# Attention stage of a hybrid decoder trunk: TensorE's instruction order fixed as the program is recorded, projections dealt anew over the steps

## The chip, the core and the metric

The kernel runs on one core of one Trainium2 chip. The metric is the device time of one execution in microseconds (us). An engine is named as the profile names it: PE is TensorE's matmuls, PEld its weight loads, DVE is VectorE, ACT ScalarE, POOL GpSimd, SP the queue that issues DMAs.

## What is computed

One layer of a trunk: adaLN-modulated RMSNorm, one input projection, two groups of 8 heads of 64 (an RWKV-7 recurrence and a causal stick-breaking attention), a gate on each, an output projection, residual and final RMSNorm, for 2048 tokens of width 1024 in float32. The change lies in the attention group:

```python
def block(args):                       # 128 queries of one head against all keys
    z = jnp.einsum('bhqd,bhkd->bhqk', q_blk, k).astype(jnp.float32) * scale
    mask = k_pos[None, :] < q_pos[:, None]
    log_1m = jnp.where(mask, jax.nn.log_sigmoid(-z), 0.0)
    after = lax.cumsum(log_1m, axis=3, reverse=True) - log_1m
    attn = jnp.where(mask, jnp.exp(jax.nn.log_sigmoid(z) + after), 0.0)
    return jnp.einsum('bhqk,bhkd->bhqd', attn.astype(v.dtype), v)
...
h = rmsnorm(x, norm_g[l]) * (1.0 + scale[:, None, :]) + shift[:, None, :]
p = h @ w_in[l]                        # q, k, v, the gates and the RWKV inputs
```

## The kernel before

The program has three parts in time. The first normalizes and transposes the input into `hth` and `htl` (high and low halves in fp16), the second is the attention, the third the RWKV recurrence and the output projection. Only the second is touched, and the end of the first.

**The attention is 16 steps.** Step n = 4j + b works on head pair j (4 pairs) and query block b (4 blocks of 512 rows); a group below is the four steps of one j. In a step there are 8(b+1) tiles of 128 queries by 512 keys, 8 of them on the diagonal and narrower. Per tile:
- `scores` (L506, L507): two matmuls into a PSUM bank z (3 banks); ACT makes two sigmoids u and s of it; DVE runs a scan over u (L519, L522); POOL multiplies s by it.
- `turn` (L535): four transposes of s into a bank tr (2 banks); ACT copies it to ah (L539), DVE takes the remainder al (L540).
- `weigh` (L553, L554): two matmuls by v add ah and al into the bank av (1 bank).

`attend` issues `scores` of a tile LEAD = 5 tiles ahead of its `turn`, and `weigh` LAG = 3 tiles behind.

**Beside it, `fill` makes the projections.** A projection is 24 matmuls of 512 columns (`inproj`; 96 of 128 columns for v) into one PSUM bank "mm", of which the stage has one. ACT and then DVE read the bank before the next projection may start. psk, psq, psv, psg and pss are the names of that bank by what is projected: k, q, v, a gate, an RWKV input. For q, ACT writes the high half (L419) and DVE the low half (L420) of the tile qt, and three DMAs (L422 to L424) move halves between partitions; the third overwrites what the first reads. `scores` of head 0 reads what the third wrote. `w_load` fetches the next projection's weights into a buffer "raw" (one of it) and takes their maximum on DVE (wm, L319); `w_split` scales and splits them, with a small matmul wtp (L333).

**What sets the order.** `_merge` interleaves `attend` and `fill` by the shares of work that their `yield`s name. That is the order of recording. The attention's context then has a scheduler (`schedule_with_timeline_sim=True`) that moves instructions on every engine by its own estimate; the engines run what comes out in order. Before the change nothing held TensorE to the order of recording, except that from step 12 on each first matmul of a k-step comes after the latest `weigh` (`pace`). Steps with b = 0 do not look ahead into the next step, and a step with b = 1 begins with five `scores`.

Of the kernel before, what the change touches and what calls it, by code (L numbers as in the profile page):

```python
# [7 lines left out]
F32 = mybir.dt.float32  # L8
# [10 lines left out]
P = 128  # L19
# [69 lines left out]
def trunk(nc, a, out):  # L89
# [7 lines left out]
    w_in, ada_w, w_out = a["w_in"][0], a["ada_w"][0], a["w_out"][0]  # L97

    base = -(-nc.sbuf_base // 32) * 32
    words = 23848  # L100
# [40 lines left out]
    crow = cp.tile([8, P], F32, name="crow")  # L141
# [12 lines left out]
    rows = cp.tile([P, P], F32, name="rows")  # L154
    col = {}
    r0 = 0
    for i, (nm, ap, off, n) in enumerate(vecs):
# [33 lines left out]
            xs.append(xt)  # L191
        xblk[b] = xs

    sbk = stage.enter_context(ExitStack())
    kp = sbk.enter_context(tc.tile_pool(name="kv", bufs=1))
    xctx = ExitStack()
# [128 lines left out]
    def w_split(kind, j):  # L325
        raw, m1 = W[kind, j]
        wh = wp.tile([P, KB, P], F16, tag="wh", name="wh")
        wl = wp.tile([P, KB, P], F16, tag="wl", name="wl")

        dg = wl.rearrange("p k c -> p (k c)")[:, 0:2 * P].bitcast(F32)  # L330
        A.activation(out=dg, in_=ident, func=AF.Copy, scale=m1)
        tp = tr_ps("wtp")
# [12 lines left out]
        rk = sm.tile([P, KB, 1], F32, name="rkw")  # L345
        V.tensor_scalar(out=rk[:, :, 0], in0=his, scalar1=ws, scalar2=None, op0=ALU.mult)
        (V if kind == "k" and j == 0 else G).tensor_tensor(out=raw, in0=raw, in1=_bc(rk, [P, KB, P]), op=ALU.mult)
        A.activation(out=wh, in_=raw, func=AF.Copy)
        V.tensor_tensor(out=wl, in0=raw, in1=wh, op=ALU.subtract)
        W[kind, j] = (wh, wl, uns)  # L350
        m = WCOL[kind][1]
        if m is not None:
            um = wp.tile([P, 1], F32, tag="um", bufs=8, name="um")
            u1 = wp.tile([P, 1], F32, tag="u1", bufs=8, name="u1")
            V.tensor_tensor(out=um, in0=uns, in1=vec("mu", 1, m + j), op=ALU.mult)
            V.tensor_tensor(out=u1, in0=uns, in1=mu1[:, m + j:m + j + 1], op=ALU.mult)
            W[kind, j] += (um, u1)
# [2 lines left out]
        w_load(kind, j, True)  # L360
        _run(w_split(kind, j))

    pace = [None]
# [12 lines left out]
    def inproj_tok(w, b, name):  # L376
        wh, wl = w[0], w[1]
        ps = mm_ps(name)
        for i in range(4):
            t = slice(i * P, (i + 1) * P)  # L380
            for k in range(KB):
                PE.matmul(ps[:, t], hth[b][:, k, t], wh[:, k], start=k == 0, stop=False)
                PE.matmul(ps[:, t], hth[b][:, k, t], wl[:, k], start=False, stop=False)
                PE.matmul(ps[:, t], htl[b][:, k, t], wh[:, k], start=False, stop=k == KB - 1)
                if k % 4 == 3:
                    yield 0.65
        return ps
# [73 lines left out]
    def combine(j, b, pool):  # L461
# [10 lines left out]
        yield 0.45  # L472
        tp = tr_ps()
        with tc.issue_after(first[0]) if first else nullcontext():
            for q in range(4):
# [19 lines left out]
    def scores(n, i, sb):  # L495
# [7 lines left out]
        nk = (q + 1) * P if diag else TB  # L503
        qs = slice(q * P, (q + 1) * P)
        z = z_ps()
        PE.matmul(z[:, 0:nk], qt[:, h, 0, qs], kt[:, h, 0:nk], start=True, stop=False)  # L506
        PE.matmul(z[:, 0:nk], qt[:, h, 1, qs], kt[:, h, 0:nk], start=False, stop=True)  # L507
# [20 lines left out]
    def turn(n, i, sb):  # L528
# [3 lines left out]
        q0 = ks if groups[gi][1] == b else 0  # L532
        tp = tr_ps()
        for q in range(q0, 4):
            PE.transpose(tp[:, q * P:(q + 1) * P], att[gi, q][:, ks * P:(ks + 1) * P], ident)  # L535
# [7 lines left out]
    def weigh(sb, n, i, ah, al, r):  # L543
# [9 lines left out]
        PE.matmul(av[:, r], vs, ah[:, r], start=first, stop=False, skip_group_check=True)  # L553
        ins = PE.matmul(av[:, r], vs, al[:, r], start=False, stop=last, skip_group_check=True)  # L554
        if n >= 12:
            pace[0] = ins.ins
        if last:

            if h == 0:
# [76 lines left out]
    w_load("g", 0, True)  # L636
    _merge((make_hs(*range(2, NB)), 3.6 * (NB - 2)), (proj_qkv(1), 15.6), (w_split("g", 0), 0.3))
    gate_row()
    xctx.close()
    cz = [zero1]  # L640

# [4 lines left out]

    def fill(n, sb):

        j, b = divmod(n, NB)
        end = j == NB - 1  # L650
        if n < 2:
            m = n + 2
        else:
            m = n + 1 if 2 < n < NST - 1 else None
        new = b == 3 and not end
        if b == 0 and j > 0:
            yield from w_split("g", j)
# [3 lines left out]
        if b == 3:  # L661
            yield from w_split("z" if end else "k", 0 if end else j + 1)
            w_load("rk" if end else "q", 0 if end else j + 1)
        gates = [("g", 0)], [("g", 1)], [("g", 2), ("g", 3), ("r", 0)], [("r", 1), ("r", 2), ("r", 3)]
        gates = [proj_g(kind, j, gb, sb) for kind, gb in gates[b]]
        if m is not None:
            yield from proj_k(m)
            if new:
                yield from gates.pop(0)
                yield from w_split("q", j + 1)  # L670
                w_load("v", j + 1)
            yield from proj_q(m)
            if new:
                yield from gates.pop(0)
                yield from w_split("v", j + 1)
                w_load("g", j + 1)
            yield from proj_v(m)
        if j > 0:
            yield from combine(j - 1, b, sb)
        if n == NST - 1:  # L680
            for i in range(4):
                yield from proj_z(i, sb)
                if gates:
                    yield from gates.pop(0)
                if i < 3:
                    yield from w_split(("rk", "rr", "rv")[i], 0)
                if i < 2:
                    w_load(("rr", "rv")[i], 0)
        for g in gates:
            yield from g  # L690
        if b == 1:
            w_load("r", j)

    def fill_work(n):
        b = n % NB
        if n == NST - 1:
            return 5.2 * 7 + 1.5
        return 5.2 * ((4, 4, 6, 6)[b] - 3 * (n == 2)) + 0.9 * (n > 3) + (0.2, 0, 0.2, 0.6)[b]

    dts = []  # L700
    early[0] = False
    with tc.tile_pool(name="sb", bufs=2) as sb:
# [7 lines left out]
        for n in range(NST):  # L710
            b = n % NB
            _merge((attend(n, sb), 8.6 + 10.48 * b), (fill(n, sb), fill_work(n)))
            if n == 1:
# [3 lines left out]
                for i in range(2):  # L717
                    dts.append(dram(f"dt{i}", [2, 2, 8, 65, 64]))
                    for m in range(2):
                        for h in range(2):  # L720
                            DMA.dma_start(out=dts[i][m, h].rearrange("c s t -> s c t")[0:64],
                                          in_=zeros[0:64].rearrange("p (c d) -> p c d", c=8))
    sbk.close()
    pace[0] = None


    HS = [slice(0, 64), slice(64, 128)]
# [608 lines left out]
```

## Time and profile before

| | |
|---|---|
| three runs | 1912.26, 1912.5 and 1915.36 us; median 1912.5 |
| the profiled execution | 1910.53 us, of which the span (first to last instruction) is 1908.8 |
| first `scores` / last `weigh` of the attention | 129.8 / 1034 us from the span's start |
| first matmul of the third part | 1044.9 us |
| PE, DVE, ACT, POOL busy over the span | 1719.8 (90%), 1348.7 (71%), 870.0 (46%), 754.6 (40%) us |
| mean granted TensorE clock | 0.971 of full speed |

All times of rows are microseconds from the span's start. A busy PE is one with a matmul in flight; matmuls overlap, so a row's duration is longer than the spacing of two matmuls. The granted clock has two levels, 2.4 GHz (1.00) and 1.2 GHz (0.50); a stretch shows their mean.

### The profile page before, as it was taken

To read this page: it belongs to the slowest core of one execution; us is meant where nothing else is said; L and a number is where in the kernel's file an instruction comes from. 1 tells how busy PE (TensorE), PEld (TensorE's weight loads), DVE (VectorE), ACT (ScalarE), POOL (GpSimd) and SP (SyncE) were. 2 spreads that over 40 slices of the span, in tenths; PEclk is the share of its full clock that TensorE was granted. 3 is DMA by queue.
4 is the path that set the end of the run, shared out by engine and by line. 5 is a ranking of instruction groups with operands and counts; after the bars stand their busy time and mean duration, and the time that the engine had idled before them with its cause. 6 is when DMAs were issued, how large, how long until landed. Compare 5 with 4: busy or idle time off the path is not lost. (4 is left out here: it accounts for less than half of the span.)

```text
span 1908.8 us, 38922 instructions
## 1 busy us (share of the span) xinstructions
PE 1719.8 (90%) x14880; PEld 1161.5 (61%) x14880; DVE 1348.7 (71%) x2855; ACT 870.0 (46%) x1718; POOL 754.6 (40%) x1106
## 2 busy tenths in 40 slices
PE   7979889999899998999997898898899888989998
PEld 2646556666566665667654455665555565667886
DVE  4876788577776778768775667877877777775542
ACT  2665567366654656546654333323332333422221
POOL 1425466355643646445444223222223232223322
PEclk9889999999999999999998899999999999999999
DMA  8442201222123221132111423222333333236442
GB/s 298 150 116 56 56 26 50 64 64 70 37 56 81 67 56 42 51 92 67 45 50 56 133 55 83 68 60 74 77 81 81 80 77 107 75 94 179 149 138 89
DMA packets 210408, 159.93 MB, mean 84 GB/s; under 512 B 113247, under 2 KB 171820, under 8 KB 210222
## 3 DMA queue, kind: packets, MB, share of 16 engines
q1 hardware_dynamic: 209220, 155.31, 29.2%
q8 instruction: 117, 1.92, 0.4%
q10 hardware_dynamic: 1002, 2.13, 0.4%
q14 instruction: 69, 0.57, 0.1%
HBM read 94.48 MB, written 44.04 MB: 73 GB/s over the span
## 5 line engine op out<-in xcount | busy, mean ns | idle before, releaser
L523 POOL TENSOR_TENSOR s<-s,u 128x512 f32<-128x512 f32 (+2 forms) x320 | 305.8, 963 | 216.5 <-ACT s L511 102.0
L540 DVE TENSOR_TENSOR al<-tr,ah 128x512 fp32r<-128x512 f32 (+1 forms) x320 | 187.4, 599 | 96.3 <-ACT ah L539 95.7
L522 DVE TENSOR_TENSOR_SCAN u<-u,dmask 128x512 f32<-128x512 f32 x192 | 240.0, 1268 | 13.0 <-ACT u L510 11.4
L539 ACT ACTIVATE ah<-tr 128x512 fp32r<-128x512 f32 (+1 forms) x320 | 171.7, 553 | 103.7 <-PE tr L535 99.6
L510 ACT ACTIVATE u<-z 128x512 f32<-128x512 f32 (+2 forms) x320 | 173.4, 555 | 73.4 <-PE z L507 49.0
L535 PE MATMUL tr<-kept_ident,s 128*128 128x128 f32 x1088 | 173.5, 279 | 33.1 <-DVE al L540 26.5
L511 ACT ACTIVATE s<-z 128x512 f32<-128x512 f32 (+2 forms) x320 | 166.2, 549 | 53.0 <-PE tr L535 53.0
L535 PEld LDWEIGHTS tr<-kept_ident,s 128*128 128x128 f32 x1088 | 130.3, 143 | 74.9 <-DVE al L540 38.4
L370 PE MATMUL pss<-kept_hh,kept_wh 128*128 128x512 f16 x416 | 161.3, 388 | 8.8 <-PEq L730 8.8
L372 PE MATMUL pss<-kept_hh,kept_wl 128*128 128x512 f16 x416 | 160.9, 387 | 0.0
L371 PE MATMUL pss<-kept_hl,kept_wh 128*128 128x512 f16 x416 | 160.9, 387 | 0.0
L372 PEld LDWEIGHTS <-kept_wl 128*128 128x128 f16 x928 | 93.2, 100 | 104.9 <-issue 14.2
L370 PEld LDWEIGHTS <-kept_wh 128*128 128x128 f16 x928 | 94.3, 102 | 101.4 <-issue 29.2
L371 PEld LDWEIGHTS <-kept_wh 128*128 128x128 f16 x928 | 93.0, 100 | 94.8 <-issue 25.0
L506 PE MATMUL z<-kt,qt 128*128 128x512 f32 (+2 forms) x320 | 132.1, 417 | 9.5 <-issue 3.7
L553 PE MATMUL av<-ah,vt 128*128 128x512 f32 (+1 forms) x320 | 136.5, 427 | 3.9 <-DVE o L564 2.3
L554 PE MATMUL av<-al,vt 128*128 128x512 f32 (+1 forms) x320 | 136.0, 426 | 0.2 <-DVE al L540 0.2
L507 PE MATMUL z<-kt,qt 128*128 128x512 f32 (+2 forms) x320 | 117.5, 371 | 0.0
L519 DVE TENSOR_TENSOR_SCAN u<-u,dmask 128x128 f32<-128x128 f32 (+3 forms) x128 | 107.3, 867 | 11.6 <-ACT u L510 6.6
L370 PE MATMUL psg<-kept_hh,kept_wh 128*128 128x512 f16 x256 | 99.1, 387 | 10.9 <-DVE klo L434 4.8
L1274 PE MATMUL po<-kept_woh,kept_yh 128*128 128x512 f32 x256 | 102.3, 400 | 0.0
L1275 PE MATMUL po<-kept_wol,kept_yh 128*128 128x512 f32 x256 | 101.5, 397 | 0.0
(296 smaller groups left out, 4146.1 us busy)
## 6 DMA issues: line engine op xcount, KB each, us to landing
kept_raw<-in_w_in SPq DMA_DIRECT2D x29, 512.0 KB, 4.3
ad<-in_ada_w SPq DMA_DIRECT2D x24, 512.0 KB, 5.6
qt<-qt SPq DMA_DIRECT2D x48, 256.0 KB, 3.3
xt<-in_x SPq DMA_DIRECT2D x16, 512.0 KB, 5.1
y<-sg SPq DMA_DIRECT2D x32, 256.0 KB, 2.3
t<-dt SPq DMA_DIRECT2D x64, 128.0 KB, 3.2
xr<-in_x SPq DMA_DIRECT2D x16, 512.0 KB, 3.6
out<-xr SPq DMA_DIRECT2D x16, 512.0 KB, 2.6
```

The lines of the kernel that those rows point to most:

```text
L370: PE.matmul(ps, wh[:, k], hth[b][:, k], start=k == 0, stop=False)
L371: PE.matmul(ps, wh[:, k], htl[b][:, k], start=False, stop=False)
L372: PE.matmul(ps, wl[:, k], hth[b][:, k], start=False, stop=k == KB - 1)
L510: A.activation(out=u[:, 0:nk], in_=z[:, 0:nk], func=AF.Sigmoid, scale=-0.125)
L511: A.activation(out=s[:, 0:nk], in_=z[:, 0:nk], func=AF.Sigmoid, scale=0.125)
L522: V.tensor_tensor_scan(out=ur, data0=ur, data1=mr, initial=u[:, nk:nk + 1], op0=ALU.mult, op1=ALU.bypass)
L523: G.tensor_tensor(out=s[:, 0:nk], in0=s[:, 0:nk], in1=u[:, 1:nk + 1], op=ALU.mult)
L535: PE.transpose(tp[:, q * P:(q + 1) * P], att[gi, q][:, ks * P:(ks + 1) * P], ident)
L539: A.activation(out=ah[:, r], in_=tp[:, r], func=AF.Copy)
L540: V.tensor_tensor(out=al[:, r], in0=tp[:, r], in1=ah[:, r].bitcast(F32), op=ALU.subtract)
L553: PE.matmul(av[:, r], vs, ah[:, r], start=first, stop=False, skip_group_check=True)
L554: ins = PE.matmul(av[:, r], vs, al[:, r], start=False, stop=last, skip_group_check=True)
```

## The change

- **Order.** Every matmul and transpose of `inproj`, `inproj_tok`, `scores`, `turn` and `weigh` is put on a list (`pin`) as it is recorded. At the end of the attention each is made to follow the one before it on the list (`pinned`). `pace` is gone. The small matmuls (wtp, the transposes of `finish` and `combine`) are not on the list.
- **Depth.** LEAD 5 to 6, LAG 3 to 2, ten s and six u buffers instead of eight and five; two small tiles move to a pool that is freed early, which makes room.
- **Look-ahead.** `attend` always looks six tiles ahead, over every step's end. Where the next step's q is not recorded yet, it yields until it is.
- **Deal.** The projections of steps b = 0, 1, 2, 3 are 3, 4, 6 and 7 (before 4, 4, 6, 6), and behind each `fill` yields 0.8 us of share. `w_split` yields 1.2 more before its matmul, `combine` 2.4 instead of 0.45 before its transposes.

```diff
+    def pinned():
+        for p, i in zip(order, order[1:]):
+            tc.add_manual_dep(i, p.name, mybir.DependencyInfo(mybir.DependencyClass.NoSync,
...
-            with tc.issue_after(pace[0]) if pace[0] is not None else nullcontext():
-                PE.matmul(ps, wh[:, k], hth[b][:, k], start=k == 0, stop=False)
-            PE.matmul(ps, wh[:, k], htl[b][:, k], start=False, stop=False)
-            PE.matmul(ps, wl[:, k], hth[b][:, k], start=False, stop=k == KB - 1)
+            pin(PE.matmul(ps, wh[:, k], hth[b][:, k], start=k == 0, stop=False))
+            pin(PE.matmul(ps, wh[:, k], htl[b][:, k], start=False, stop=False))
+            pin(PE.matmul(ps, wl[:, k], hth[b][:, k], start=False, stop=k == KB - 1))
...
-    NS, NU, LEAD, LAG = 8, 5, 5, 3
+    NS, NU, LEAD, LAG = 10, 6, 6, 2
...
-        ahead = LEAD if n % NB else 0
-        if n % NB == 1 or n == 0:
+        if n == 0:
             for p in range(p0, p0 + LEAD):
                 yield scores(*seq[p], sb)
         for p in range(p0, p1):
-            if p + LEAD < min(p1 + ahead, len(seq)):
+            if p + LEAD < len(seq):
+                while seq[p + LEAD][0] not in qst:
+                    yield 0.02
                 yield scores(*seq[p + LEAD], sb)
...
+        def paused(gen):
+            yield from gen
+            yield 0.8
+        def kqv(m):
+            yield from paused(proj_k(m))
+            yield from paused(proj_q(m))
+            yield from paused(proj_v(m))
+        if b == 0:
+            if j > 0:
+                yield from w_split("g", j)
+            w_load("r", j)
+            if j > 0:
+                yield from kqv(n + 1)
+            else:
+                yield from paused(proj_k(2))
+                yield from paused(proj_v(2))
+                yield from paused(proj_q(2))
...
+        return 6.0 * ((3, 4, 6, 7)[b] - 3 * (n == 2)) + 2.85 * (j > 0) + (1.5, 0, 1.5, 4.4)[b]
```

**Place 1, PE, where step 4 (j = 1, b = 0) projects q of step 5.** After the change, numbers tell one tile from another: psq_3985 is the bank, qt_3984 the tile that is made from it, s and tr are step 4's.

```order
L384 MATMUL psq_3985<-kept_hl40416_514,kept_wh7584_290 128x512
L385 LDWEIGHTS kept_wl9632_291
L385 MATMUL psq_3985<-kept_hh32224_513,kept_wl9632_291 128x512
L520 MATMUL z_4015<-kt_3910,qt_3984 128x128
L521 MATMUL z_4015<-kt_3910,qt_3984 128x128
L549 MATMUL tr_4026<-kept_ident0_61,s_3762 128x128
L549 MATMUL tr_4026<-kept_ident0_61,s_3790 128x128
L395 LDWEIGHTS kept_hh32224_513
L395 MATMUL psv_4034<-kept_wh11712_316,kept_hh32224_513 128x128
```

Before, at the same place, q (qt_3942) is projected, then come 15 instructions of step 4's `weigh` and `turn`, the whole of v (96 matmuls), and only then the first `scores` with that q; these are the last rows of that stretch.

```order
L383 MATMUL psv_4022<-kept_wl14784_314,kept_hh33248_510 128x128
L384 LDWEIGHTS kept_hl41440_511
L384 MATMUL psv_4022<-kept_wh12736_313,kept_hl41440_511 128x128
L535 MATMUL tr_4140<-kept_ident0_61,s_3907 128x128
L535 MATMUL tr_4140<-kept_ident0_61,s_3951 128x128
L506 MATMUL z_4204<-kt_3878,qt_3942 128x128
L507 MATMUL z_4204<-kt_3878,qt_3942 128x128
```

The first `scores` of step 5 has moved ahead of v, directly behind q's last matmul. The same stands at steps 8 and 12. At the ends of the other steps at least one whole projection stands between.

**Place 2, DVE, at the same place after the change.** klo is k's low half, kept_wl the low half of weights that `w_split` makes, wm the maximum over weights that a new `w_load` fetched into the buffer that kept_wl was made from.

```order
L447 SCALAR_TENSOR_TENSOR klo_3978<-psk_3911,kept_uns93728_2854,kt_3910 128x512
L352 TENSOR_TENSOR kept_wl67040_826<-kept_raw85504_1240,kept_wh64992_825 128x1024
L590 TENSOR_REDUCE ssq_3968<-on_3966 128x8
L591 TENSOR_SCALAR ssq_3968<-ssq_3968 128x8
L320 TENSOR_REDUCE wm_3905<-kept_raw85504_1240 128x8
L321 TENSOR_TENSOR wm_3905<-wm_3905,kept_his2016_230 128x8
L433 SCALAR_TENSOR_TENSOR qt_3984<-psq_3985,kept_uns93760_3025,qt_3984 128x512
```

q's low half stands behind wm, as it did before; the matmul wtp that begins the chain to kept_wl now stands in k's sixth k-step instead of ahead of k's first.

**Place 3, PE, between k and q of step 6 (b = 2), after the change.**

```order
L385 MATMUL psk_4855<-kept_hh69088_1012,kept_wl5504_265 128x512
L549 MATMUL tr_4949<-kept_ident0_61,s_4733 128x128
L567 MATMUL av_4930<-ah_4876,vt_4489 128x384
L568 MATMUL av_4930<-al_4877,vt_4489 128x384
L520 MATMUL z_4963<-kt_3040,qt_4383 128x512
L521 MATMUL z_4963<-kt_3040,qt_4383 128x512
L383 LDWEIGHTS kept_wh7584_290
L383 MATMUL psq_4974<-kept_hh69088_1012,kept_wh7584_290 128x512
```

Before, between the same two projections (these rows are the whole of it but for the 3 transposes and one `weigh` matmul that follow):

```order
L372 MATMUL psk_4857<-kept_hh70112_1011,kept_wl6528_262 128x512
L506 MATMUL z_4904<-kt_3878,qt_4341 128x512
L507 MATMUL z_4904<-kt_3878,qt_4341 128x512
L535 MATMUL tr_4861<-kept_ident0_61,s_4693 128x128
L535 MATMUL tr_4861<-kept_ident0_61,s_4719 128x128
L535 MATMUL tr_4861<-kept_ident0_61,s_4747 128x128
L535 MATMUL tr_4861<-kept_ident0_61,s_4775 128x128
L506 MATMUL z_4948<-kt_2871,qt_4341 128x512
L507 MATMUL z_4948<-kt_2871,qt_4341 128x512
L506 MATMUL z_4981<-kt_2871,qt_4341 128x512
L507 MATMUL z_4981<-kt_2871,qt_4341 128x512
L553 MATMUL av_4709<-ah_4818,vt_3496 128x512
```

The attention's instructions have moved out of the spaces between projections into the projections: a projection was some 24 matmuls nearly without a break, and now has one tile's `scores`, `turn` or `weigh` after every k-step or two.

## Rows read from the trace of the kernel before

**Rows 1.** Windows, cut at last `weigh` of steps: us, busy PE PEld DVE ACT POOL, PEclk, DMA, GB/s

```profile
206.60:263.10 56.50, 46.87 (x243) 31.99 (x242) 45.76 (x66) 38.15 (x83) 33.03 (x60) 0.97 0.09 29
263.10:352.40 89.30, 80.31 (x492) 54.24 (x491) 70.72 (x108) 54.25 (x113) 51.52 (x83) 0.98 0.16 44
...
381.70:429.80 48.10, 48.07 (x330) 33.21 (x328) 36.16 (x53) 29.06 (x65) 26.38 (x50) 1.00 0.24 65
429.80:490.20 60.40, 58.09 (x384) 39.85 (x382) 48.58 (x68) 40.20 (x85) 33.87 (x61) 1.00 0.22 59
490.20:582.70 92.50, 82.08 (x496) 55.69 (x496) 72.96 (x110) 54.42 (x113) 50.64 (x83) 0.96 0.17 48
582.70:610.20 27.50, 23.76 (x200) 17.08 (x199) 13.93 (x24) 10.38 (x26) 7.36 (x16) 1.00 0.40 101
```

**Rows 2.** Waits of PE, 206.6 to 352.4: waited for, total, times, longest

```profile
PE tr L535 <- DVE al L540: 8.5, 9, 1.4
PE psg L370 <- DVE sg L456: 3.3, 1, 3.3
PE psg L370 <- DVE klo L434: 2.1, 1, 2.1
```

**Rows 3.** Waits of PE, 490.2 to 582.7 (first two), and 381.7 to 490.2

```profile
PE tr L535 <- DVE al L540: 5.6, 5, 2.2
...
PE psg L370 <- DVE klo L434: 1.4, 1, 1.4
...
PE psv L382 <- DVE qt L420: 0.4, 1, 0.4
```

**Rows 4.** Timeline of PE at step 12: start, us, what, [idle before <-releaser]

```profile
812.79 0.38 PE L370 MATMUL psq<-kept_hh,kept_wh 128*128 128x512 f16 x1 [1.74 <-DVE klo L434]
...
817.32 0.60 PE L572 MATMUL otp<-kept_ident,o 128*128 128x128 f32 x4
...
818.29 0.38 PE L372 MATMUL psq<-kept_hh,kept_wl 128*128 128x512 f16 x1
...
821.69 0.22 PE L382 MATMUL psv<-kept_wh,kept_hh 128*128 128x128 f16 x1 [0.34 <-DVE qt L420]
...
829.25 0.30 PE L506 MATMUL z<-kt,qt 128*128 128x128 f32 x1 [1.82 <-issue]
```

**Rows 5.** Timeline of the same place, the engines that q's tile passes through

```profile
803.32 0.38 PE L333 MATMUL wtp<-kept_wl,kept_ones 128*128 128x128 f32 x2
...
812.10 0.41 SPq L317 DMA_DIRECT2D kept_raw<-in_w_in  x1
...
817.57 1.22 DVE L319 TENSOR_REDUCE wm<-kept_raw 128x8 f32<-128x1024 f32 x1 [3.67 <-DMA kept_raw<-in_w_in]
...
820.16 0.69 ACT L419 ACTIVATE qt<-psq,kept_uns 128x512 fp32r<-128x512 f32 x1
...
820.88 0.75 DVE L420 SCALAR_TENSOR_TENSOR qt<-psq,kept_uns,qt 128x512 fp32r<-128x512 f32 x1 [0.29 <-ACT qt L419]
...
821.66 0.46 SPq L422 DMA_DIRECT2D qt<-qt  x1
...
825.86 0.46 SPq L424 DMA_DIRECT2D qt<-qt  x1
```

**Rows 6.** Windows around the start of the third part, columns as in Rows 1

```profile
1038.00:1042.00 4.00, 0.00 (x0) 0.00 (x0) 0.75 (x2) 0.00 (x0) 2.68 (x2) 0.50 0.00 0
...
1047.00:1049.00 2.00, 2.00 (x6) 0.71 (x5) 0.00 (x0) 0.47 (x1) 0.43 (x2) 0.50 0.76 228
```

**Rows 7.** Timeline of PE, two `scores` in a row at full clock

```profile
607.87 0.39 PE L506 MATMUL z<-kt,qt 128*128 128x512 f32 x1
...
608.33 0.39 PE L506 MATMUL z<-kt,qt 128*128 128x512 f32 x1
```

**Rows 8.** Windows: tile psq before the attention (PE DVE ACT, PEclk); its first 7.8 us

```profile
98.00:129.80 31.80, 5.51 (x24) 0.75 (x1) 0.67 (x1) 0.84 0.55 161
...
129.80:137.60 7.80, 5.18 (x19) 3.88 (x18) 3.98 (x7) 4.79 (x15) 3.39 (x16) 0.68 0.00 1
```

More of the change, by code (lines that the diff above doesn't have):

```diff
@@ L99, in trunk @@
     base = -(-nc.sbuf_base // 32) * 32
-    words = 23848
+    words = 23592
     ctx.enter_context(nc.sbuf_tensor("kept", [P, words], F32))
@@ L139, in trunk @@
     V.tensor_copy(out=id2[64:128], in_=ident[64:128, 64:128])
-    crow = cp.tile([8, P], F32, name="crow")
+    sbk = stage.enter_context(ExitStack())
+    kp = sbk.enter_context(tc.tile_pool(name="kv", bufs=1))
+    xctx = ExitStack()
+    rowp = xctx.enter_context(tc.tile_pool(name="rows", bufs=1))
+    crow = rowp.tile([8, P], F32, name="crow")
     DMA.dma_start(out=crow, in_=a["c"][0].rearrange("(r c) -> r c", c=P))
@@ L153, in trunk @@
     V.tensor_tensor(out=cact, in0=cact, in1=cps[:, 0:8], op=ALU.mult)
-    rows = cp.tile([P, P], F32, name="rows")
+    rows = rowp.tile([P, P], F32, name="rows")
     col = {}
@@ L331, in w_split @@
         A.activation(out=dg, in_=ident, func=AF.Copy, scale=m1)
+        yield 0.6
+        yield 0.6
         tp = tr_ps("wtp")
@@ L361, in w_prep, with pin @@
         _run(w_split(kind, j))
-    pace = [None]
+    order = []
+    def pin(ins):
+        order.append(ins.ins)
+    def pinned():
+        for p, i in zip(order, order[1:]):
+            tc.add_manual_dep(i, p.name, mybir.DependencyInfo(mybir.DependencyClass.NoSync,
+                                                              mybir.DependencyReason.DATA), reason="order")
+        order.clear()
     def inproj(w, b, name):
@@ L381, in inproj_tok @@
             for k in range(KB):
-                PE.matmul(ps[:, t], hth[b][:, k, t], wh[:, k], start=k == 0, stop=False)
-                PE.matmul(ps[:, t], hth[b][:, k, t], wl[:, k], start=False, stop=False)
-                PE.matmul(ps[:, t], htl[b][:, k, t], wh[:, k], start=False, stop=k == KB - 1)
+                pin(PE.matmul(ps[:, t], hth[b][:, k, t], wh[:, k], start=k == 0, stop=False))
+                pin(PE.matmul(ps[:, t], hth[b][:, k, t], wl[:, k], start=False, stop=False))
+                pin(PE.matmul(ps[:, t], htl[b][:, k, t], wh[:, k], start=False, stop=k == KB - 1))
                 if k % 4 == 3:
@@ L471, in combine @@
         DMA.dma_start(out=sg, in_=ydram[4 + j][b])
-        yield 0.45
+        for _ in range(1 if pool is None else 3):
+            yield 0.8
         tp = tr_ps()
@@ L505, in scores @@
         z = z_ps()
-        PE.matmul(z[:, 0:nk], qt[:, h, 0, qs], kt[:, h, 0:nk], start=True, stop=False)
-        PE.matmul(z[:, 0:nk], qt[:, h, 1, qs], kt[:, h, 0:nk], start=False, stop=True)
+        pin(PE.matmul(z[:, 0:nk], qt[:, h, 0, qs], kt[:, h, 0:nk], start=True, stop=False))
+        pin(PE.matmul(z[:, 0:nk], qt[:, h, 1, qs], kt[:, h, 0:nk], start=False, stop=True))
         u = sb.tile([P, TB + 1], F32, tag="u", bufs=NU, name="u")
@@ L552, in weigh @@
         vs = vst[NB * j + kb][:, ks, h].rearrange("p l d -> p (l d)")
[L553 to L556, printed above, removed]
+        pin(PE.matmul(av[:, r], vs, ah[:, r], start=first, stop=False, skip_group_check=True))
+        pin(PE.matmul(av[:, r], vs, al[:, r], start=False, stop=last, skip_group_check=True))
         if last:
@@ L638, in trunk @@
     gate_row()
+    order.clear()
     xctx.close()
@@ L650, in fill, with g @@
         end = j == NB - 1
[L651 to L657, printed above, removed]
+        def paused(gen):
+            yield from gen
+            yield 0.8
+        def g(kind, gb):
+            return paused(proj_g(kind, j, gb, sb))
+        def kqv(m):
[12 more added lines that the diff above has]
+                yield from paused(proj_q(2))
+        if b == 1:
+            if j > 0:
+                yield from kqv(n + 1)
+                yield from g("g", 2)
+            else:
+                yield from paused(proj_k(3))
+                yield from paused(proj_v(3))
+                yield from g("g", 3)
+                yield from paused(proj_q(3))
         if b == 2:
@@ L660, in fill @@
             w_load("z" if end else "k", 0 if end else j + 1)
[L661 to L677, printed above, removed]
+            if j > 0:
+                yield from kqv(n + 1)
@@ new lines, in fill @@
+            yield from g("g", 3 if j > 0 else 2)
+            yield from g("r", 3)
+            yield from g("r", 2)
+        if b == 3 and not end:
+            yield from w_split("k", j + 1)
+            w_load("q", j + 1)
+            yield from g("g", 1)
+            yield from w_split("q", j + 1)
+            w_load("v", j + 1)
+            yield from paused(proj_k(n + 1))
+            yield from w_split("v", j + 1)
+            w_load("g", j + 1)
+            yield from paused(proj_q(n + 1))
+            yield from paused(proj_v(n + 1))
+            yield from g("g", 0)
+            yield from g("r", 0)
+            yield from g("r", 1)
@@ new lines, in fill @@
+        if b == 3 and end:
+            yield from w_split("z", 0)
+            w_load("rk", 0)
+            yield from g("g", 1)
+            yield from paused(proj_z(0, sb))
+            yield from paused(proj_z(1, sb))
+            yield from g("r", 1)
+            yield from w_split("rk", 0)
+            w_load("rr", 0)
+            yield from g("g", 0)
+            yield from g("r", 0)
+            yield from w_split("rr", 0)
+            w_load("rv", 0)
+            yield from paused(proj_z(2, sb))
+            yield from w_split("rv", 0)
+            yield from paused(proj_z(3, sb))
@@ L678, in fill, with fill_work @@
         if j > 0:
             yield from combine(j - 1, b, sb)
+    def fill_work(n):
+        j, b = divmod(n, NB)
         if n == NST - 1:
[L681 to L698, printed above, removed]
+            return 6.0 * 8 + 5.6
+        return 6.0 * ((3, 4, 6, 7)[b] - 3 * (n == 2)) + 2.85 * (j > 0) + (1.5, 0, 1.5, 4.4)[b]
     dts = []
@@ L722, in trunk @@
                                           in_=zeros[0:64].rearrange("p (c d) -> p c d", c=8))
+    pinned()
     sbk.close()
-    pace[0] = None
     HS = [slice(0, 64), slice(64, 128)]
```

5 lines of the change are left out of this document (1 added, 4 removed).

## The prediction

> **What bounds the kernel now.** I read the windows first, cut at the last `weigh` of each step, because a mean over the span hides that the steps differ. Five of the windows of the second group and the end of the first are [rows 1]; the third and fourth groups repeat them within 2 us a step. The reader is to see three kinds of step. In b = 1 (381.7 to 429.8) PE stands still for nothing: 48.07 of 48.10. In b = 2 it loses 2.3 of 60.4. In b = 3 it loses 92.5 - 82.1 = 10.4, and its clock is granted at 0.96, so half rate for 8% of the stretch, another 3.7. DVE is busy 73.0 of those 92.5, so no engine is full: the time goes into waits for each other. In the first group (206.6 to 352.4) PE loses 9.6 and 9.0, and 1.7 and 1.8 to the clock. The waits say for what: in b = 3 transposes for al, 5.6, and a projection for the bank's eviction, 1.4 [rows 3]; in the first group 8.5 and 5.4 [rows 2]. These are waits of bunches: PE runs a projection, then several `turn`s in a row, and the third `turn` finds both tr banks in DVE's hands. The third part is not touched, so the sum is about the attention alone, some 10.4 + 3.7 + 2.3 = 16.4 us a group at b = 2 and 3 that could be won at most.
>
> **The change, part by part.** I work per group and take three full groups and the first by itself.
>
> *(a) The score behind q.* At steps 4, 8 and 12 PE now stops at the first `scores` of the next step until q has been evicted and moved by DMA, and v, which covered that, is queued behind it. What the chain takes is in [rows 5]: ACT 0.69, DVE 0.75, then from the first DMA's issue at 821.66 over the third's at 825.86 (it waits for the first two to land) to the `scores` at 829.25 [rows 4] 7.6. With the hand-overs 9.1 from q's last matmul. That is the lower bound. It is longer if DVE is late: wm stands ahead of q on DVE and waits for a weight load. In this trace the load took 5.5 from issue to wm (812.10 to 817.57), and the load was issued 8.8 after wtp. Now wtp stands 3 k-steps ahead of k's end, some 2.3 us. If the 8.8 were kept, the load would be issued 6.5 after k's end, wm would end at 6.5 + 5.5 + 1.4 = 13.4, and q, ready for DVE at about 7.7 (a bank wait of 1.6, 5.3 for 24 matmuls [rows 8], ACT), would be 5.7 late. That is the upper bound, 14.8. Half of the 8.8 in this trace is other DVE and POOL work, so I take 3 late: 12 us. Before, PE waited 1.82 and 0.34 at the same place [rows 4]; the wait of q for k's bank, 1.74 there, stays and is left out. A long stop also costs clock: in the one long stop of the trace PE did nothing from 1038 to 1042 and was at 0.50 still at 1047 to 1049, after it had started again at 1044.9 [rows 6]; some 4 us at half rate lose 2 (bounds 1 and 3). So 12 - 2.2 + 2 = +11.8 a group, bounds +8 and +15.6. **Three times: +35.**
>
> The Trainium skill ("DMA: Bandwidth & Descriptors", section "Anatomy of one DMA") gives a fit of about 2.0 us fixed plus bytes at 436 GB/s for one transfer, fitted on the other issue path. An estimate by it for two transfers of 256 KB behind each other is 5.2, against 7.6 in the rows, and the sum would be 7 lower. The measurement decides, and the sum goes by the rows.
>
> *(b) The bank between projections.* ACT and DVE must read the one bank before the next projection. At the least that takes 0.69 + 0.75 and hand-overs, 1.5; at q of step 12 it took 3.0 (818.7 to 821.63 [rows 4, 5]). Before, the scheduler put `scores`, `turn` and `weigh` between (place 3 of the order: six `scores` matmuls, seven transposes, a `weigh`, some 2.6 us). Now 12 of a group's 20 spaces hold only 0.7 to 1.4 us, mean 1.05 (a pair of `scores` is 0.46 [rows 7], four transposes under 0.6 [rows 4], a `weigh` as a pair of `scores`). The wait for each is between 0.45 and 1.95; most evictions fall where ACT and DVE are less than full, so I take 0.75, near the lower end. 12 x 0.75 = 9, less the 1.8 waited for banks before [rows 3]: +7 a group, bounds +3.5 and +20. **Three times: +21.** In steps 2 and 3 only four spaces are short.
>
> *(c) The bunches.* Spread over the k-steps, a `turn` has two tiles' worth of PE work between it and the one that used its bank, where it had about one. In b = 3 a tile then has 2.5 us of PE work, and DVE has 73.0 / 32 = 2.3 for it, so little is to be waited for but where `fill` pauses and attention stands alone. Of the 16.4 in b = 2 and 3, 1.8 are bank waits, counted in (b). Of the 14.6 left I take 2 to stay: -12.5 a group, bounds -14.6 and -6 (the al waits alone [rows 3]). **Three times: -37.** LEAD, LAG and the buffers are in this: LEAD 6 with 10 s buffers only feeds it.
>
> *(d) The first group.* Steps 2 and 3 lose 9.6 + 9.0 + 3.5 = 22 now [rows 1]. I leave 5 in step 2 (DVE has 45.8 of work there, and PE 45 with the new deal), 3 in step 3, and 2 for banks: -12, bounds -18 and -4. Against it, step 0: k and q of block 2 were projected before the first `scores`, in a stretch in which PE waits for loads anyway: 24 matmuls, 5.5 us, each [rows 8], 10.4 in matmul time for both. They now follow the first `scores`. 2.5 come back because that starts earlier, and 5 because the first 7.8 us of the attention, 5.2 busy at clock 0.68 [rows 8], get filled; bank waits of 2 come on top: +5, bounds 0 and +12. **Together -7.**
>
> The deal moves one projection, 5.2, from b = 0 to b = 3 and costs nothing by itself: PE's work of a group is the same, and b = 3's DVE has the room just named; without the room each would cost its 0.75 of DVE.
>
> Sum: +35 + 21 - 37 - 7 = +12. Against the profiled execution, 1910.5, that is **1923 us**; against the median, 1912.5, it would be 1925, and I do not split 2 us. The measurement tells 0.2%, 4 us, from no change.
>
> **The rivals.**
> - *Faster.* The interleave takes out all bunches and evictions are short. For it: b = 1 already runs without a wait, with spaces like the new ones. Against it: b = 1 has the lightest DVE load (36 of 48). Price: (a) +30, (b) +13, (c) -43, (d) -14, sum -14, and with (a) at its lower bound -20 to -27: about 1888. It decides when a group wins more in (c) than (a) and (b) lose, that is from about 19 won less lost banks.
> - *Banks decide.* ACT and DVE run in a fixed order, and an eviction stands behind a scan or a copy whose input PE, itself waiting, has not made. For it: 3.0 in [rows 4, 5] and the 3.3 wait of [rows 2]. Against it: waits that short on average before. Price: 12 x 1.6 a group instead of 12 x 0.75, +31: about 1953.
> - *A wash, or the order does not change.* The order was read, and it does change; but the four terms, each 7 to 37, can cancel: 1910 to 1916.
>
> **How the numbers follow.** The forecast case, 1917 to 1940: 0.36. Faster: 0.36, of which little lies below 1885. Banks: 0.14. Wash: 0.14. The range from 1885 to 1955 leaves out about 2 in 10: half of it beyond 1955 with the upper bounds of (a) and (b), half below. By sign: faster by over 0.2% 0.36, within 0.2% 0.14, slower 0.50. The forecast case's own range is 1917 to 1940.
>
> **What would show it.** (a) in PE's waits three stops of 9 to 15 us at `scores` for q's DMA, right behind the last matmul of psq, and half clock behind them; wm ahead of q on DVE ended by the weight load. (b) some 50 waits of a projection's first matmul for the low half on DVE, 0.5 to 1.5 each. (c) in b = 3 under 3 us of transposes waiting for al, and PE busy 95% of the rest. (d) the first `scores` at 126 to 129, step 3 ended 8 us earlier than 352.4. The prediction is wrong if the stop behind q is hidden, or if the attention's b = 3 steps still take 90 us, or 80.

## The result: the changed kernel takes 2010 us, 4.9% more, and all of it lies in the attention

The changed kernel takes 2009.98 us (median of 4 runs, 2005.4 to 2012.56) against 1912.38 us before (4 runs, 1912.15 to 1915.36), 97.6 more; the ratio of the two is given as 1.0488, 95% interval 1.0461 to 1.0515. The forecast was 1923 us, with a range that ended at 1955. The profiled execution took 2005.4 us, 94.9 more than the profiled one before. Of the four runs of e12_before_z2 (below), one took 4265 us; the median and the ratio there are those of the other three.

These are windows of the changed kernel, steps 2 to 4, 7 and 8, cut at the last `weigh` of each step, with the columns of [rows 1].

```profile
208.60:260.70 52.10, 47.81 (x265) 32.88 (x264) 48.60 (x71) 38.62 (x82) 34.40 (x62) 1.00 0.12 37
260.70:358.90 98.20, 85.26 (x510) 56.96 (x509) 72.00 (x109) 55.71 (x112) 50.20 (x83) 0.97 0.16 45
358.90:402.20 43.30, 29.60 (x200) 20.82 (x198) 18.77 (x28) 15.45 (x32) 14.22 (x23) 0.80 0.27 71
...
518.20:622.10 103.90, 88.35 (x514) 58.72 (x513) 74.20 (x114) 56.12 (x113) 49.51 (x83) 0.93 0.16 45
622.10:662.60 40.50, 26.43 (x200) 18.93 (x198) 18.64 (x28) 15.23 (x32) 14.23 (x23) 0.87 0.29 75
```

Step 3 ends 6.5 us later than before, although the attention starts 5.2 earlier. Then the group of steps 4 to 7 (358.9 to 622.1) takes 263.2 us where it took 230.3 (352.4 to 582.7 in [rows 1]). Step 8 (b = 0) was 27.5 in [rows 1] and takes 40.5, with 139 matmuls of projections in its window where there were 145; step 7 (b = 3) was 92.5 and takes 103.9, with 256 in place of 240. DVE is hardly busier than before, 74.2 against 73.0 in step 7. So no engine became full; PE stands more.

What it stands for is in PE's waits over the whole attention. First the changed kernel, then the kernel before; columns: what waited, for what, total, times, longest.

```profile
PE wtp L336 <- ACT kept_wl L332: 25.1, 5, 7.6
PE z L520 <- issue: 20.4, 2, 10.2
PE tr L549 <- DVE al L554: 12.9, 18, 1.2
PE psq L383 <- DVE klo L447: 11.8, 11, 2.4
PE psv L395 <- DVE qt L433: 11.2, 9, 2.8
PE z L520 <- DMA qt<-qt: 10.5, 1, 10.5
PE otp L584 <- DVE o L576: 8.5, 14, 2.1
PE av L567 <- DVE o L576: 8.1, 6, 2.1
PE psg L383 <- DVE sg L469: 7.2, 9, 1.3
...
PE tr L549 <- DVE sgl L492: 3.4, 3, 1.1
```

```profile
PE tr L535 <- DVE al L540: 26.5, 27, 2.2
PE psq L370 <- DVE klo L434: 5.2, 3, 1.7
PE psg L370 <- DVE klo L434: 4.8, 3, 2.1
PE otp L572 <- DVE o L564: 4.3, 3, 1.4
PE z L506 <- issue: 3.7, 2, 1.8
```

And these are the windows of the whole attention, the changed kernel first:

```profile
124.60:1130.30 1005.70, 863.70 (x5391) 580.42 (x5391) 688.89 (x1003) 550.83 (x1124) 477.87 (x837) 0.95 0.19 51
```

```profile
129.80:1034.10 904.30, 832.74 (x5347) 569.18 (x5347) 677.78 (x1004) 534.65 (x1124) 469.72 (x836) 0.98 0.21 56
```

The window grew by 101.4 us, and PE's busy time by 31.0. Of these 31.0, some 10.4 (the prediction's figure for them) are k and q of block 2, which now lie behind the first `scores`; the other 20.6 are the same matmuls taking longer. Most of that is clock: cut into windows of 1 us, PE was busy at half clock for some 34 us before and 64 after, and an estimate from these is that a full clock would save half of each, 17 and 32. The rest fits with a tile's matmuls now alternating with a projection's: the first `scores` matmul of a full tile has a mean of 507 ns, 448 before, the second 399 in both. PE's idle time grew by 101.4 - 31.0 = 70.4:

| PE waits at | before | after |
|---|---|---|
| wtp, for a weight's maximum | 0 | 25.1 |
| `scores`, for q's transfers | 5.6 | 30.9 |
| a projection's first matmul, for the bank | 18.0 | 47.2 |
| step ends (otp, av for o, tr for sgl) | 6.6 | 20.0 |
| `turn`, for al | 26.5 | 12.9 |

These are sums over the rows of each kind, those not shown included. Of the row for q's transfers the profile puts two stops down to "issue"; all three are the first `scores` behind q, at 376.6, 640.2 and 896.0. Together they rose by 79.4, and the small rest fell by some 9. The 96.2 by which the attention ends later (1130.3 against 1034.1) are 101.4 less the 5.2 of the earlier start.

The largest new row of waits for one instruction is one that the prediction did not have. This is the timeline of wtp in step 7, k's first and q's last (start, duration, idle before and releaser):

```profile
516.97 0.38 PE L336 MATMUL wtp<-kept_wl,kept_ones 128*128 128x128 f32 x2
...
523.91 2.01 DVE L352 TENSOR_TENSOR kept_wl<-kept_raw,kept_wh 128x1024 f16<-128x1024 f32 x1 [1.61 <-ACT kept_wh L351]
...
525.95 0.38 SPq L318 DMA_DIRECT2D kept_raw<-in_w_in  x1
...
530.31 1.26 DVE L536 TENSOR_TENSOR_SCAN u<-u,dmask 128x512 f32<-128x512 f32 x1
...
531.50 1.19 DVE L320 TENSOR_REDUCE wm<-kept_raw 128x8 f32<-128x1024 f32 x1
...
533.90 0.40 ACT L332 ACTIVATE kept_wl<-kept_ident,m 128x128 f32<-128x128 f32 x1 [5.64 <-DVE m L323]
534.36 0.79 PE L336 MATMUL wtp<-kept_wl,kept_ones 128*128 128x128 f32 x2 [7.64 <-ACT kept_wl L332]
```

There is one raw buffer. q's weights can be fetched only when k's have been split out of it (525.95), their maximum begins 5.5 us later, behind a scan on DVE that ends as it starts, and then comes the small matmul. k's own wtp ran from 516.97 to 517.35, so the chain takes 17.4 us (534.36 - 516.97), and the order holds only 18 matmuls of a gate and the attention's tiles between the two. PE is through with them 9.7 us after k's wtp, at 526.7, and stands 7.64 us, although k's projection, next in the order, needs nothing of it; the clock is at 0.50 from 531.5 to 538.3 (windows below). Before, no wait at wtp shows in the attention.

The stop that was forecast is there too, at 640.2 in step 8:

```profile
629.32 0.38 PE L385 MATMUL psq<-kept_hh,kept_wl 128*128 128x512 f16 x1
629.74 0.69 ACT L432 ACTIVATE qt<-psq,kept_uns 128x512 fp32r<-128x512 f32 x1 [4.05 <-PE psq L385]
630.66 1.22 DVE L320 TENSOR_REDUCE wm<-kept_raw 128x8 f32<-128x1024 f32 x1 [2.38 <-DMA kept_raw<-in_w_in]
...
632.00 0.75 DVE L433 SCALAR_TENSOR_TENSOR qt<-psq,kept_uns,qt 128x512 fp32r<-128x512 f32 x1
...
632.77 0.47 SPq L435 DMA_DIRECT2D qt<-qt  x1
637.21 0.46 SPq L437 DMA_DIRECT2D qt<-qt  x1
640.21 0.44 PE L520 MATMUL z<-kt,qt 128*128 128x128 f32 x1 [10.51 <-DMA qt<-qt]
```

wm stands ahead of q on DVE and makes it 1.5 us late; from the first DMA to `scores` it is 7.4 (7.6 in [rows 4, 5]). The windows of half clock at both stops, this one first:

```profile
633.90:644.10 10.20, 3.89 (x29) 3.85 (x30) 0.90 (x2) 0.83 (x3) 0.74 (x3) 0.50 0.46 104
531.50:538.30 6.80, 3.94 (x14) 2.69 (x15) 4.14 (x11) 1.00 (x2) 4.86 (x4) 0.50 0.15 41
```

Each lasts some 4 us beyond its stop, with PE busy at half rate.

### The profile page after: what moved, and what is told of

It reads as the page before. It is cut to its first block, busy times and chain, and to the rows that moved or that the text cites. A ratio compares the mean times of both kernels' runs of the same rounds, so it can differ in the third digit from the quotient of the medians.

```text
span 2003.5 us, 39061 instructions
## 1 busy us (share of the span) xinstructions
PE 1739.0 (87%) x14880; PEld 1167.6 (58%) x14880; DVE 1358.0 (68%) x2855; ACT 884.9 (44%) x1718; POOL 761.6 (38%) x1106
## 5 line engine op out<-in xcount | busy, mean ns | idle before, releaser
L536 DVE TENSOR_TENSOR_SCAN u<-u,dmask 128x512 f32<-128x512 f32 x192 | 245.1, 1276 | 101.5 <-ACT u L524 93.4
L549 PE MATMUL tr<-kept_ident,s 128*128 128x128 f32 x1088 | 180.4, 282 | 20.1 <-DVE al L554 12.9
L533 DVE TENSOR_TENSOR_SCAN u<-u,dmask 128x128 f32<-128x128 f32 (+3 forms) x128 | 111.5, 876 | 114.8 <-ACT u L524 108.5
L520 PE MATMUL z<-kt,qt 128*128 128x512 f32 (+2 forms) x320 | 152.7, 477 | 31.7 <-issue 20.4
L525 ACT ACTIVATE s<-z 128x512 f32<-128x512 f32 (+2 forms) x320 | 171.6, 536 | 0.0
L549 PEld LDWEIGHTS tr<-kept_ident,s 128*128 128x128 f32 x1088 | 136.0, 145 | 59.6 <-DVE al L554 12.3
L567 PE MATMUL av<-ah,vt 128*128 128x512 f32 (+1 forms) x320 | 163.0, 509 | 8.4 <-DVE o L576 8.1
L384 PEld LDWEIGHTS <-kept_wh 128*128 128x128 f16 x928 | 93.9, 101 | 74.2 <-issue 40.6
L568 PE MATMUL av<-al,vt 128*128 128x512 f32 (+1 forms) x320 | 119.2, 372 | 0.0
L521 PE MATMUL z<-kt,qt 128*128 128x512 f32 (+2 forms) x320 | 118.6, 371 | 0.0
L395 PE MATMUL psv<-kept_wh,kept_hh 128*128 128x128 f16 x512 | 98.8, 229 | 14.9 <-DVE qt L433 11.2
```

The source lines that it names most:

```text
L384: pin(PE.matmul(ps, wh[:, k], htl[b][:, k], start=False, stop=False))
L525: A.activation(out=s[:, 0:nk], in_=z[:, 0:nk], func=AF.Sigmoid, scale=0.125)
L536: V.tensor_tensor_scan(out=ur, data0=ur, data1=mr, initial=u[:, nk:nk + 1], op0=ALU.mult, op1=ALU.bypass)
L549: pin(PE.transpose(tp[:, q * P:(q + 1) * P], att[gi, q][:, ks * P:(ks + 1) * P], ident))
L567: pin(PE.matmul(av[:, r], vs, ah[:, r], start=first, stop=False, skip_group_check=True))
```

## The experiments

The theory after the result (A): TensorE is held to the order of recording, so a late input stops everything behind it; the loss is the stop behind q, the stop at wtp and the waits for the one bank, with the slower matmuls that come with them. Each kernel was timed beside the kernel before on the same chip, which took 1917 to 1919 us in these runs; gains are given as the difference of two ratios times 1917.

| kernel | us, median | ratio to before, 95% interval |
|---|---|---|
| e1_hold_v | 1984.26 | 1.0356 [1.0324, 1.0388] |
| e2_cover_q | 1997.15 | 1.0420 [1.0385, 1.0455] |
| e3_both | 1976.03 | 1.0299 [1.0273, 1.0326] |
| e4_unpinned | 1927.22 | 1.0044 [1.0023, 1.0066] |
| e5_two_banks | 1975.37 | 1.0299 [1.0273, 1.0324] |
| e6_pause | 1992.41 | 1.0375 [1.0336, 1.0415] |
| e7_depth | 2012.9 | 1.0509 [1.0477, 1.0540] |
| e8_all | 1943.3 | 1.0132 [1.0076, 1.0188] |
| e9_pin_attn | 1956.44 | 1.0192 [1.0158, 1.0225] |
| e11_z2 | 1949.86 | 1.0172 [1.0129, 1.0215] |
| e12_before_z2 | 1883.18 | 0.9821 [0.9767, 0.9875] |
| e13_all_z2 | 1908.56 | 0.9962 [0.9939, 0.9985] |
| e14_cover | 1977.77 | 1.0320 [1.0287, 1.0352] |
| e15_free | 1909.31 | 0.9947 [0.9924, 0.9971] |
| e16_q_first | 1906.09 | 0.9947 [0.9927, 0.9968] |

**e1_hold_v: v back between q and its scores.**

```diff
-                while seq[p + LEAD][0] not in qst:
+                while seq[p + LEAD][0] not in qst or seq[p + LEAD][0] not in vst:
```

> Attention waits with its look-ahead until the next step's v is recorded, not only its q, so v's 96 matmuls stand again between q's last matmul and the first scores at steps 4, 8 and 12. Theory A (the stops for q's transfers, 10.2, 10.5 and 10.2 us, and the half clock behind them, 9.5 us in the three steps, are paid in full): the three stops are gone, some 4 us a step come back as waits of six tiles in a row behind v, time 1970 to 1982. Rival (the tiles queued behind the stop wait for ACT and DVE anyway): the stop's time turns up as waits for al and s, time 2000 to 2010.

25 us less than the change, just above the time expected. The waits of `scores` for q's transfers fell from 30.9 to 4.7, but v now begins right behind q, and its waits for q's bank rose from 11.2 to 20.6. The stop was real; part of it came back at the one bank.

**e2_cover_q and e14_cover: more projections between the weights' splits.**

```diff
             yield from g("g", 1)
+            yield from g("g", 0)
             yield from w_split("q", j + 1)
             w_load("v", j + 1)
             yield from paused(proj_k(n + 1))
+            yield from g("r", 0)
             yield from w_split("v", j + 1)
```

The first + alone is e2, both are e14 (the two gates stood at the end of the step).

> In steps with b = 3 a second gate (g, block 0) is projected ahead of the split of q's weights instead of at the end. Theory A (the small matmul wtp of q's weights stands in PE's queue 8.8 us of PE work behind that of k's weights, while its chain by multiply, two copies, load and maximum takes 17.4): with 19 us of PE work between them the waits of 7.6, 7.6 and 8.8 us go, and most of the 11.8 us that half clock costs in these steps: 1975 to 1985. Rival (the chain is late for other reasons, and the wait moves to the next wtp or to the kernel's next projections): 2003 to 2012.

> The change with two gates between the splits of k's and q's weights, and now also one between the projections of k and q, ahead of v's split; the one bank and the look-ahead as in the change. Theory A (the stops at wtp cost their 25 us and the half clock behind them, some 5; the cover of q's weights alone had moved a stop of 6 to v's): 1975 to 1985. Rival (the order of weights is not the cause, the wait moves again): 1993 to 2005, as with the one gate.

e2 gave 13 us: q's wtp was covered, and a wait of 6.1 appeared at v's, which now had too little ahead of it; the rival was partly right. With both covers the waits at wtp are 1.9 and the gain is 32, as expected. This is the window of step 7 in e14_cover:

```profile
508.70:600.80 92.10, 84.80 (x515) 57.03 (x513) 73.62 (x114) 55.62 (x113) 49.11 (x83) 0.98 0.18 51
```

92.1 against 103.9 above, for nearly the same matmuls (515 and 514), with the clock at 0.98 for 0.93.

**e3_both: e1 and e2 together.** 

> Both edits together. Theory A: the two gains add, 1938 to 1955; what is left above the kernel before (26 to 43) is waits for the one projection bank (47 us against 18) and for the step's end (finish, o: 17 against 7). Rival (either stop hides the other's wait): the sum is under two thirds of the two single gains.

36 less, where the single gains sum to 38: they add. The expected time was too low, because e2's gain had been put at 25 to 35.

**e4_unpinned: the list thrown away (`pinned()` becomes `order.clear()`).**

> Everything of the change except the pin: the list is thrown away and the scheduler orders TensorE as it did before. Theory A (what costs is that TensorE is held to the order of recording, where a wait stops everything behind it): the scheduler puts v ahead of the first scores and wtp late, 1905 to 1940. Rival B (the new deal, the look-ahead and the depth cost by themselves): 1980 to 2010.

85 us less, 0.44% above the kernel before. With one bank, the new deal, look-ahead, pauses and depth cost little if the scheduler orders; the order does the harm. One part of the loss is not wholly the pin's: wtp was never on the list, the scheduler chooses its place, and it still waits 8.8 at it here, where it waited 25.1.

**e9_pin_attn: only `scores`, `turn` and `weigh` pinned**, `pin(...)` taken off in `inproj` and `inproj_tok`.

> Only scores, turn and weigh are put on the list; the projections' matmuls are left to the scheduler. Theory A (what costs is that projections are fixed between the tiles, so that a late bank, a late weight or q's transfer stops all behind it): 1915 to 1945, bank and wtp waits under 25 us together. Rival (the fixed order of attention itself, six ahead and two behind, makes the loss): 1970 to 2010.

Between the two: 57 less than the change, 28 above the free order, so theory A's time was missed, though the waits for the bank and at wtp together came to 19, under the 25 expected. The stops at q and wtp are gone (3.9 and 1.3), but projections now wait some 28 for the two halves of their weights; what in attention's fixed order makes the scheduler place them so early was not tried.

**e7_depth: `NS, NU, LEAD, LAG = 8, 5, 5, 3`.**

> Depth as in the kernel before: five tiles ahead, sums three behind, eight s and five u buffers; order still pinned, deal and pauses of the change. Theory A (depth has little to do with the loss): 2000 to 2016. Rival (two behind, with three buffers for ah and al, is what makes PE wait): under 1990.

Unchanged within the two intervals. Six ahead and two behind are not the cause.

**e6_pause: 2.4 in place of 0.8 behind each projection.**

> Pauses of 2.4 in place of 0.8 behind each projection, one bank as before; more of attention's tiles then stand between two projections and fewer inside one. Theory A: a space of about 2 us of PE work covers most of an eviction, bank waits 47 to about 25 us, time 1985 to 1995. Rival (the tiles bunch again in the spaces, and al waits grow by as much): 2003 to 2015.

22 less. The bank waits fell further than expected, to 14.7, but `weigh` behind a step's end now waits 20.3 for o, where it waited 8.1. Part of the wait moved.

**e5_two_banks and e11_z2: a second bank for projections.** 

```diff
-    NM = [1, 3, 2]
+    NM = [2, 2, 2]
```

This is e11, which takes the bank from the scores. e5 takes it from the scans' mask, which moves to SBUF.

> The change with two banks for projections in place of one (the mask of the scans moves from PSUM to SBUF; ten s buffers become nine and six tiles ahead become five, to make room). Theory A (the one bank costs what PE's waits of a projection's first matmul sum to, 47 us in the attention): they fall under 12 us, the stops at scores and at wtp stay: 1965 to 1980. Rival (ACT and DVE are late as such, and the waits turn up at the transposes and scores): 1995 to 2010.

> The change with two banks for projections and two for scores in place of one and three; the mask stays in PSUM, ten s, six ahead. Theory A (a second projection bank is worth what the waits for the one are, 47 us, and the scan keeps its 1.28 us): 1955 to 1975. Rival (scores need the third bank; PE then waits at scores for ACT's sigmoids): 1985 to 2010.

e5 gave 36, e11 61. In both no wait for a bank is left, and in e11 `scores` waits 1.8 for a sigmoid: the third score bank had hardly been needed. e11's gain is more than the 47.2 of waits: PE's idle time fell by 39.7, since other waits grew (those for q's transfers from 30.9 to 35.0), and its busy time by 863.70 - 843.19 = 20.5 us for the same matmuls, some 13 of it less half clock by the estimate above (waits, then the window of the attention):

```profile
PE wtp L336 <- ACT kept_wl L332: 25.7, 5, 7.6
PE z L520 <- issue: 23.5, 2, 11.8
...
PE z L520 <- DMA qt<-qt: 11.5, 1, 11.5
```

```profile
124.70:1070.20 945.50, 843.19 (x5391) 569.33 (x5391) 685.68 (x1003) 549.36 (x1124) 476.55 (x837) 0.96 0.20 54
```

The Trainium skill ("Perfetto Trace Analysis", section "Matmuls") says that independent groups of matmuls should rotate through several banks, so that the eviction of one lies beside the next. The runs agree: 61 us here, and 34 us in the kernel before (e12_before_z2).

**e8_all and e13_all_z2: the three causes taken away, still pinned** (e1, e14 and a second bank; e8 with e5's bank, e13 with e11's).

> The three causes taken away together, the order still pinned: look-ahead held until v is recorded, two gates between the splits of k's and q's weights and one between q's and v's, two banks for projections (mask in SBUF, nine s, five ahead). Theory A (stop behind q, wtp stop and bank waits, with the clock behind them, are the loss): from 1975 with two banks, less 25 for the stop behind q and 25 for wtp: 1918 to 1932. Rival (each stop taken away uncovers another wait in the pinned order, as the cover of q's weights did with v's): 1940 to 1960.

> As e8_all, but the second projection bank is taken from the scores, the mask stays in PSUM, ten s, six ahead. Theory A: 1905 to 1930, about 10 under e8_all since the scans stay 0.23 us shorter each. Rival (third score bank needed): over 1940.

e13 takes 1908.56: 101 less than the change and 0.4% less than the kernel before, in the same fixed order. e8 stayed above its range, in the rival's; its mask in SBUF makes the scans longer (below), and al waits are 32.3. What e13 still waits for:

```profile
PE tr L549 <- DVE al L554: 19.4, 24, 1.9
PE z L520 <- issue: 12.6, 2, 6.4
PE av L567 <- DVE o L576: 10.6, 10, 2.1
PE z L520 <- DMA qt<-qt: 7.1, 1, 7.1
```

`scores` waits 6 to 7 again at each b = 0: with a second bank, v runs at once behind q and is over after 5.5, while q's chain takes some 12.

**e15_free and e16_q_first: is there a price left on the pin, and on that stop?** e15 is e13 without the pin; in e16 steps with b = 0 project q, k, v in place of k, q, v.

> The kernel of two projection banks and two score banks with look-ahead held for v and the gates moved, without the pin. Theory A (the pin costs only through the long waits, and those are gone): within 0.7% of the pinned one's 1908.6, 1895 to 1922. Rival B (a free order is better by itself, as with the kernel before at two and two banks): 1875 to 1890.

> As the pinned kernel with two and two banks, holds and gates, but in steps with b = 0 q is projected first, then k, then v, so that two projections stand between q and its first scores. Theory A (the 7 us that scores still wait for q's transfers at each such step is q's chain of 12 less v's 5.2): those waits fall from 19.8 to under 6 us, 1890 to 1900. Rival (k's transfers are then the last, and scores wait for them instead): 1904 to 1915.

e15 and e13 agree within their spread: with the long waits gone the pin costs nothing that can be measured. e16 moved the wait to k's transfers (4.5 in one row, 5.4 in another of two stops) and to the transposes of `combine` (8.7), and saved no more than the spread: the rival.

**e12_before_z2: the kernel before with `NM = [2, 2, 2]`.**

> The kernel before with two banks for projections and two for scores, order left to the scheduler. Theory A (waits for the one bank, 18.9 us in the attention before, are real there too): 1895 to 1908. Rival (a scheduler that fills the spaces needs score banks more): 1912 to 1935.

1.8% less than the kernel before, more than expected, and the fastest of all. The windows of steps 7 and 8 show where it comes from; against the 92.5 and 82.08 of [rows 1] step 7 has more matmuls in the same time, PE is never idle in step 8, and the clock stays up:

```profile
472.80:565.20 92.40, 86.28 (x526) 55.76 (x526) 71.10 (x108) 54.72 (x113) 48.89 (x82) 1.00 0.20 52
565.20:591.00 25.80, 25.80 (x212) 18.23 (x210) 17.21 (x32) 12.18 (x27) 14.16 (x23) 1.00 0.41 108
```

## Why the prediction was wrong, by its own steps

- **(a) The score behind q: +35.** Right in place and size. Waits rose by 25.3 (5.6 to 30.9), and steps 4 and 8, with 200 matmuls each before and after though not quite the same ones, held 4.1 and 2.7 of busy time more (25.46 and 23.76 before, 29.60 and 26.43 after); half clock is an estimated 3.7 and 2.0 of it, where 2 a step were taken. The stop is 10.2 to 10.5 us, between the bounds of 9.1 and 14.8; wm delayed q by 1.5 where 3 was taken. Taking it away returned 25, after 9.4 more of waits for q's bank.
- **(b) The bank between projections: +21.** Right in place, somewhat small. The waits rose by 29.2, to 46 waits of 1.0 on average. The price of the one bank is more than its waits, 61 us by e11_z2, a third of it shorter busy time; but 34 of it the kernel before pays too (e12_before_z2), so the difference, which the step priced, is 26. Its upper bound of +20 a group is +21.6 by its own figures (12 x 1.95 - 1.8).
- **(c) The bunches: -37. This step failed.** That al waits would fall under 3 in b = 3 was right (2.2 in step 7, from 5.6), and over the attention they fell by 13.6. But "of the 14.6 left I take 2 to stay" booked the whole idle time and half clock of b = 2 and 3 as a prize for the interleave. Idle time in step 7 went from 10.4 to 15.6, and its clock from 0.96 to 0.93, because other waits came in: 7.6 at wtp, and 5.4 for the bank where it had been 1.4. What the interleave returned is the 13.6 of al waits, not 37.
- **The missing term.** The sum has nothing for wtp. The prediction looked at the split of the gate's weights, at b = 0, where the small matmul had moved to a harmless place, and not at b = 3, where two splits in a row share one raw buffer with one projection between them. That is 25.1 of waits, and 32 with what goes with it (e14_cover); 8.8 of the 25.1 lie in step 3, the rest in the later groups.
- **Step ends**, 13.4 more of waits for o and sgl, are also missing. With the list thrown away (e4_unpinned) these waits are 12.5, between the 6.6 before and the 20.0 after, so about half of the growth goes with the pin; what makes the rest was not tested.
- **(d) The first group: -7.** Measured +6.5 at the end of step 3. The start was 5.2 earlier, more than the 1 to 4 that was forecast (126 to 129), and step 2's idle time fell to 4.3, near the 5 left to it. Step 3's rose from 9.0 to 12.9, where 3 was left: it lost 8.8 at wtp, the missing term again.

So theory A has three parts by runs: 25 the stop behind q, 32 wtp, 61 the one bank. They sum to 118, and together they returned 101, since with the second bank some of q's stop comes back (19.7 of waits in e13, of 30.9). They are not the parts of the loss, which is 94 on the scale of these gains, for 34 of the bank's 61 is a cost that the kernel before has too. With the second bank in both kernels, the changed one with its three causes gone is still 27 us slower than the one before (e13_all_z2 against e12_before_z2); so some 67 of the 94 are the three causes, and these 27 are not. The pin is not the reason for them, since the free order (e15_free) is 24 slower too; what in the new deal, look-ahead or depth makes them, when with one bank the free order lost only 8 (e4_unpinned), was not settled. That the pin is what turns these delays into stops is shown by e4_unpinned (85), and that it costs nothing without them by e13_all_z2 beside e15_free. The rival "banks decide" put 52 on the bank, and the difference was 26 to 29; "faster" had put most on (c).

## What to carry to other kernels

A fixed order of one engine turns each input that is late by a few us into a stop of everything behind it; before fixing it, list for each small instruction on that engine (here the matmul wtp that passes on a maximum of weights) how long its chain takes and how much work stands ahead of it, above all where one buffer serves several in a row. Look at the cheapest resource first: one PSUM bank moved from scores to projections was worth 1.8% to the kernel before and 3% to the changed one, with a one-line edit. Idle time in a stage is not a prize for the edit that removes its largest wait: book only that wait's row.

## What the runs showed of the hardware that was not expected

With the scans' mask in SBUF in place of PSUM (e5_two_banks), the scan went from 1276 to 1505 ns on average, and the small GpSimd copies from 232 to 556 ns. The groups of both engines, the changed kernel first (mean ns after the busy time):

```profile
L536 DVE TENSOR_TENSOR_SCAN u<-u,dmask 128x512 f32<-128x512 f32 x192 | 245.1, 1276 | 101.5 <-ACT u L524 93.4
L535 POOL COPY u<-u 128x1 f32<-128x1 f32 x186 | 42.1, 232 | 0.0
```

```profile
L536 DVE TENSOR_TENSOR_SCAN u<-u,dmask 128x512 f32<-128x512 f32 x192 | 289.0, 1505 | 58.3 <-ACT u L524 35.5
L535 POOL COPY u<-u 128x1 f32<-128x1 f32 x192 | 106.1, 556 | 0.0
```

The Trainium skill ("GPSIMD Engine Reference", section "Specifications") says that GpSimd's SBUF interfaces are shared with VectorE, with contention when a VectorE instruction has two SBUF inputs. Both rows agree with it. That it is contention, and not the place of the mask as such, shows when the 192 scans of e5 are parted by what runs beside them: the 64 with no GpSimd instruction beside them took 1.28 us, as with the mask in PSUM; the 89 with 0.8 us or more of GpSimd beside them took 1.72 on average. With the mask in PSUM such a neighbour changed nothing (39 scans, 1.27 us). Two scans of e5 in a row, the first alone, show it; the copy that starts inside the second one takes 1.12:

```profile
178.36 1.28 DVE L536 TENSOR_TENSOR_SCAN u<-u,dmask 128x512 f32<-128x512 f32 x1
...
179.80 1.09 POOL L537 TENSOR_TENSOR s<-s,u 128x512 f32<-128x512 f32 x1 [2.05 <-DVE u L536]
180.27 1.70 DVE L536 TENSOR_TENSOR_SCAN u<-u,dmask 128x512 f32<-128x512 f32 x1
180.84 1.12 POOL L535 COPY u<-u 128x1 f32<-128x1 f32 x1
```

In this kernel a mask that costs a PSUM bank buys 0.23 us a scan on average.
